# A 3 x 3 convolution on one core: a small unused load at the head is replaced by two small stores of zeros into the output

## The chip, the core and the metric

The kernel runs on one core of a Trainium2 chip. The metric is device time in microseconds (us) of that core, and less is better. Each kernel is run several times, and the median is compared. Beside the runs there is one profiled execution, whose trace is what the profile shows; its span is the stretch from its first to its last instruction, and its time also has what lies around that.

The engines are named as the profile names them: PE (matmul) and PEld (its weight loads), DVE (vector), ACT (scalar), POOL, and SP (which only issues transfers here). A transfer (DMA) is issued by SP, ACT or POOL into a queue of its own (q1, q10 and q0 in the profile), and the same 16 DMA engines carry all of them.

## The reference

```python
x_pad = np.pad(x, ((0, 0), (0, 0), (1, 1), (1, 1)))
for b, co, ci, kh, kw in all:
    output[b, co] += weight[co, ci, kh, kw] * x_pad[b, ci, kh:kh+h, kw:kw+w]
```

There are 16 images of 64 channels, 64 x 64 pixels each, and 128 output channels, all float32. The input has 16.8 MB, the output 33.6 MB, the weights 0.29 MB.

## The kernel before, in words

Images are worked on in pairs: the 64 channels of two images fill the 128 partitions, so a pair p is one input tile of 128 x 4096 elements, and there are eight pairs. Output rows are made two at a time (even row, odd row), so that they share a product: with row weights G0, G1, G2, the kernel forms G1 times the sum of two neighbouring input rows once, and adds to it (G2 - G1) and G0 products for the even row, (G0 - G1) and G2 products for the odd row. The sums of rows are tiles `ss` (L73), the 16-bit inputs are tiles `xs`.

The head, in program order: ACT's queue loads `first` (L42), 64 bytes from each of 48 rows of the input, which nothing reads. SP's queue loads the weights `w_raw` (L44), then the first pair `x0` (L46), then the second `x1` (L48). POOL makes an identity matrix, casts the weights to 16 bits (L53), and then issues the loads of pairs 2 to 7 (L59), which cast on the way. PE transposes the weights (L91); ACT and DVE make the five weight matrices `Wt` from them (L93 to L96, L100, L101). Of `x0`, DVE makes the row sums (L73) and ACT the 16-bit copy (L98); of `x1`, POOL makes the sums and ACT the copy (L174).

The main loop runs over the eight pairs and, in each, over four blocks of 16 output rows. A block has three groups of matmuls (L154) into two PSUM tiles each (one for each image): the shared product, which ACT copies to SBUF (L168), and the two others, to which DVE adds it, into the even and odd rows of an output tile `ot` (L177, L180). The output tiles share a pool of seven buffers with `x0` and `x1`. When a pair is complete, SP stores the first image (L182, in the helper at L112), and ACT, at its next turn, the second (L171). Each is 2 MB; of the last two pairs some are stored in halves.

Calls wrapped in `keep` hold their program order. The rest is placed by the tile framework, which gives each SP and ACT transfer one of eight completion semaphores in turn, and makes a transfer wait for the one eight places earlier, which used the same semaphore. It also makes a store wait for an earlier store to the same place.

Of the kernel before, what the change touches and what calls it, by code (L numbers as in the profile page):

```python
# [8 lines left out]
F32 = mybir.dt.float32  # L9
# [4 lines left out]
def kernel(  # L14
# [6 lines left out]
    nc = tc.nc  # L21
    B, CI, H, W = x.shape
# [5 lines left out]
    keep = tc.keep_in_program_order  # L28
    x_rows = x.rearrange("b c h w -> (b c) h w")
    out_rows = out.rearrange("b co h w -> b co h w")  # L30
    w_flat = weight.rearrange("co ci kh kw -> co (ci kh kw)")

    const = ctx.enter_context(tc.tile_pool(name="const", bufs=1))
# [4 lines left out]
    upool = ctx.enter_context(tc.tile_pool(name="upool", bufs=4))  # L38


    first = const.tile([48, 16], F32)
    nc.scalar.dma_start(first, x_rows[5 * 128 :: 8, 0, 0:16])  # L42
    w_raw = const.tile([CO, CI * 9], F32)
    nc.sync.dma_start(w_raw, w_flat)  # L44
    x0 = opool.tile([128, H, W], F32, tag="ot", name="x0")
    nc.sync.dma_start(x0, x_rows[0:128, :, :])  # L46
    x1 = opool.tile([128, H, W], F32, tag="ot", name="x1")
# [169 lines left out]
```

## Time and profile before

| | |
|---|---|
| median of three runs | 127.28 us (126.99 to 127.28) |
| the profiled execution, its time | 127.19 us |
| its span | 125.4 us |
| PE, DVE, ACT, POOL busy | 84%, 67%, 36%, 28% of the span |
| queues q1 (SP), q10 (ACT), q0 (POOL): packets' time, share of 16 DMA engines | 40.7%, 31.5%, 24.6% |
| HBM read and written | 17.08 MB and 33.55 MB |

The span is read together with the queues' shares, which add up to 96.8% (q8 and q14 bring 0.3% more): the 16 DMA engines are hardly ever without a packet. The chain of waits follows the end of the work back to what released it, and the windows give, for each stretch of time, what engines and DMA did there. In a window shorter than a few us the DMA share can be over 1, since a packet is counted where it starts.

### The profile page before, as it was taken

To read this page: it belongs to the slowest core of one execution; us is meant where nothing else is said; L and a number is where in the kernel's file an instruction comes from. 1 tells how busy PE (TensorE), PEld (TensorE's weight loads), DVE (VectorE), ACT (ScalarE), POOL (GpSimd) and SP (SyncE) were. 2 spreads that over 40 slices of the span, in tenths; PEclk is the share of its full clock that TensorE was granted. 3 is DMA by queue.
4 is the path that set the end of the run, shared out by engine and by line. 5 is a ranking of instruction groups with operands and counts; after the bars stand their busy time and mean duration, and the time that the engine had idled before them with its cause. 6 is when DMAs were issued, how large, how long until landed. Compare 5 with 4: busy or idle time off the path is not lost.

```text
span 125.4 us, 2409 instructions
## 1 busy us (share of the span) xinstructions
PE 105.8 (84%) x978; PEld 53.4 (43%) x978; DVE 83.5 (67%) x134; ACT 44.5 (36%) x76; POOL 34.5 (28%) x27
## 2 busy tenths in 40 slices
PE   0407999999999999999999999999999999996000
PEld 0303445554545545554554545454554555452000
DVE  0009297787778777777787778788788878868000
ACT  4108937953333333333333333333333333331000
POOL 2840008999367005700480039000000000000000
PEclk9999999999999999999999999999999999999965
DMA  5899999999999999999999999999999999999980
GB/s 160 358 355 340 324 311 212 212 209 204 366 361 374 345 350 348 355 379 350 345 361 361 418 423 423 449 423 423 434 418 418 434 426 418 431 426 426 410 371 37
DMA packets 4106, 44.48 MB, mean 355 GB/s; under 512 B 512, under 2 KB 512, under 8 KB 640
## 3 DMA queue, kind: packets, MB, share of 16 engines
q1 hardware_dynamic: 1872, 21.27, 40.7%
q10 hardware_dynamic: 1360, 16.78, 31.5%
q0 software_dynamic: 864, 6.29, 24.6%
q8 instruction: 7, 0.11, 0.3%
q14 instruction: 3, 0.02, 0.0%
HBM read 17.08 MB, written 33.55 MB: 404 GB/s over the span
## 4 chain that ended last, share of the span: by engine, by line
PE 82%; DMA 7%; DVE 2%; issue 1%; DVEq 0%; SPq 0%
PE acc L154 82%; DMA x<-in_x_dram 7%; DVE ot L177 1%; DVE ss L73 1%; DVE ot L180 0%; DVEq L212 0%; SPq L44 0%; DVEq L177 0%
## 5 line engine op out<-in xcount | busy, mean ns | idle before, releaser
L154 PE MATMUL acc<-xs,Wt 64*128 64x504 f16 (+3 forms) x768 | 88.6, 377 | 0.0
L154 PEld LDWEIGHTS <-Wt 64*128 64x128 f16 x960 | 52.3, 95 | 56.5 <-issue 6.5
L177 DVE TENSOR_TENSOR ot<-acc,ut 128x512 f32<-128x512 f32 x64 | 41.2, 686 | 23.1 <-PE acc L154 18.5
L168 ACT COPY ut<-acc 128x512 f32<-128x512 f32 x64 | 34.4, 589 | 60.6 <-issue 40.6
L180 DVE TENSOR_TENSOR ot<-acc,ut 128x512 f32<-128x512 f32 x64 | 41.1, 685 | 0.0
L73 POOL TENSOR_TENSOR ss<-xs 128x1024 f16<-128x1024 f16 x12 | 25.2, 2128 | 29.0 <-PE acc L154 25.8
L154 PE MATMUL acc<-ss,Wt 64*128 64x504 f16 (+1 forms) x192 | 27.0, 384 | 4.5 <-DVE ss L73 4.5
L73 DVE TENSOR_TENSOR ss<-x 128x512 f16<-128x512 f32 x4 | 2.6, 685 | 9.5 <-DMA x<-in_x_dram 9.5
L73 POOL TENSOR_TENSOR ss<-x 128x1024 f16<-128x1024 f32 x2 | 4.7, 2363 | 11.6 <-DMA x<-in_x_dram 11.6
L98 ACT CAST xs<-x 128x1024 f16<-128x1024 f32 (+2 forms) x4 | 4.0, 1054 | 3.9 <-DMA x<-in_x_dram 3.9
L91 PE MATMUL wp<-ident,w 128*64 128x128 f16 x18 | 1.3, 327 | 4.5 <-POOL w L53 4.5
L174 ACT CAST xs<-x 128x1024 f16<-128x1024 f32 x4 | 4.0, 1058 | 0.0
L59 POOL DMA_DIRECT2D xs<-in_x_dram x6 | 3.4, 582 | 0.0
L91 PEld LDWEIGHTS <-w 128*64 128x64 f16 x18 | 1.1, 209 | 4.5 <-POOL w L53 4.5
L93 ACT ACT_TABLE_LOAD x1 | 1.3, 1283 | 1.2 <-PEq L201 1.2
L93 ACT CAST Wt<-wp 128x384 f16<-128x384 f32 x1 | 0.5, 479 | 2.7 <-PE wp L91 2.7
L53 POOL CAST w<-w_raw 128x576 f16<-128x576 f32 x1 | 0.7, 664 | 2.4 <-DMA w_raw<-in_weight_dram 2.4
L100 ACT CAST Wt<-wp 128x384 f16<-128x384 f32 x1 | 0.5, 480 | 0.5 <-DVE Wt L96 0.5
L95 DVE TENSOR_TENSOR Wt<-wp,Wt 128x384 f16<-128x384 f32 x1 | 0.5, 549 | 0.0
L96 DVE TENSOR_TENSOR Wt<-wp,Wt 128x384 f16<-128x384 f32 x1 | 0.5, 546 | 0.0
L101 ACT CAST Wt<-wp 128x384 f16<-128x384 f32 x1 | 0.5, 484 | 0.0
masks.py:199 POOL TENSOR_SCALAR_AFFINE_SELECT ident<-ident 128x128 f16<-128x128 f16 x1 | 0.3, 295 | 0.1
(5 smaller groups left out, 0.6 us busy)
## 6 DMA issues: line engine op xcount, KB each, us to landing
out_dram<-ot ACTq DMA_DIRECT2D x7, 2048.0 KB, 20.2
out_dram<-ot SPq DMA_DIRECT2D x6, 2048.0 KB, 20.8
xs<-in_x_dram POOLq DMA_DIRECT2D x6, 1024.0 KB, 31.0
x<-in_x_dram SPq DMA_DIRECT2D x2, 2048.0 KB, 13.0
out_dram<-ot SPq DMA_DIRECT2D x4, 1024.0 KB, 10.3
out_dram<-ot ACTq DMA_DIRECT2D x2, 1024.0 KB, 9.2
w_raw<-in_weight_dram SPq DMA_DIRECT2D x1, 288.0 KB, 3.0
first<-in_x_dram ACTq DMA_DIRECT2D x1, 3.0 KB, 2.7
```

What stands on the lines that cost most here:

```text
L53: keep(nc.gpsimd.tensor_copy(w16, w_raw))
L59: keep(nc.gpsimd.dma_start(xs[p], x_rows[128 * p : 128 * p + 128, :, :]))
L73: eng.tensor_add(ss[p][:, lo : lo + n, :], v[:, lo : lo + n, 0, :], v[:, lo : lo + n, 1, :])
L91: nc.tensor.matmul(wp[q : q + 64, k * CO : k * CO + CO], w16[:, t::9], ident)
L93: keep(nc.scalar.copy(wrow(G1), wps[1]))
L95: keep(nc.vector.tensor_sub(wrow(G21), wps[2], wrow(G1)))
L98: keep(nc.scalar.copy(xs[0][:, lo:hi, :], x0[:, lo:hi, :]))
L154: nc.tensor.matmul(tiles[b2][:, lo - j0 : hi - j0, c_lo:c_hi], Wt[p0 : p0 + 64, wi, kw, :], rhs, start=i == 0, stop=i == n - 1,)
L168: keep(nc.scalar.copy(ut, U[b2]))
L174: keep(nc.scalar.copy(xs[1][:, lo : lo + 16, :], x1[:, lo : lo + 16, :]))
L177: nc.vector.tensor_add(ots[b2][:, j0 : j0 + RB, 0, :], A[b2], us[b2])
L180: nc.vector.tensor_add(ots[b2][:, j0 : j0 + RB, 1, :], Bt[b2], us[b2])
```

## The change

`first` and its load are taken out. In its place DVE writes zeros into a tile of 128 x 16 elements, and two stores take 64 bytes from each of 16 of its partitions: ACT's queue stores to every eighth channel of the last image (15), where `first` was issued; SP's queue to every eighth channel of image 14, between the weights' load and that of the first pair. Both places are written again at the end by the stores of pair 7.

```diff
-    first = const.tile([48, 16], F32)
-    nc.scalar.dma_start(first, x_rows[5 * 128 :: 8, 0, 0:16])
+    zero = const.tile([128, 16], F32)
+    keep(nc.vector.memset(zero, 0.0))
+    nc.scalar.dma_start(out_rows[B - 1, ::8, 0, 0:16], zero[0:16, :])
     w_raw = const.tile([CO, CI * 9], F32)
     nc.sync.dma_start(w_raw, w_flat)
+    nc.sync.dma_start(out_rows[B - 2, ::8, 0, 0:16], zero[16:32, :])
     x0 = opool.tile([128, H, W], F32, tag="ot", name="x0")
     nc.sync.dma_start(x0, x_rows[0:128, :, :])
```

In the order of instructions on each engine, the changed kernel has the zeros first on DVE, one store in the load's place on ACT, and one store more on SP ahead of both input loads; PE and POOL keep their rows.

## The prediction

> **What bounds the kernel now.** I read the page's slices first, then the chain of waits, then the timeline and the windows of the head. The slices:
>
> ```profile
> PE   0407999999999999999999999999999999996000
> DMA  5899999999999999999999999999999999999980
> GB/s 160 358 355 340 324 311 212 212 209 204 366 361 374 345 350 348 355 379 350 345 361 361 418 423 423 449 423 423 434 418 418 434 426 418 431 426 426 410 371 37
> ```
>
> The DMA row is to be read before PE's: the 16 DMA engines are full from the second slice to the last but two, some 6 us longer than PE at the end. (GB/s counts bytes written, so the loads of pairs 2 to 7, which shrink to 16 bits on the way, show about half of what they read.) The chain in order of time:
>
> ```profile
> 0.74 0.38 SPq L44
> ...
> 1.17 8.32 DMA x<-in_x_dram
> ...
> 9.52 0.70 DVE ss L73
> ...
> 10.26 103.36 PE acc L154 x948
> ```
>
> After `x0` has landed PE runs 103 us without a gap. So there are two long chains, PE's and that of the DMA engines, and both begin with the transfer issued at L46. Which of them ends last? The last two stores, 1 MB each, are issued at 115.59 and 116.19 and land 8.6 and 8.3 us later, while at the 430 GB/s around them 2.1 MB take 4.9 us. There are some 3 us of other stores ahead of them: the DMA engines set the end, and PE could be 2 us late without moving it. What counts is time that DMA engines lose. The head, by timeline and windows:
>
> ```profile
> 0.74 0.38 SPq L44 DMA_DIRECT2D w_raw<-in_weight_dram  x1
> ...
> 1.17 0.42 SPq L46 DMA_DIRECT2D x<-in_x_dram  x1
> ...
> 1.65 0.42 SPq L48 DMA_DIRECT2D x<-in_x_dram  x1
> ```
>
> ```profile
> 1.50:2.00 0.50, 0.00 (x0) 0.00 (x0) 0.00 (x0) 0.50 (x1) 0.00 (x0) 1.00 0.55 60
> 2.00:2.50 0.50, 0.00 (x0) 0.00 (x0) 0.00 (x0) 0.46 (x1) 0.00 (x0) 1.00 0.65 172
> 2.50:3.00 0.50, 0.00 (x0) 0.00 (x0) 0.00 (x0) 0.00 (x0) 0.00 (x0) 1.00 1.88 618
> 3.00:3.50 0.50, 0.00 (x0) 0.00 (x0) 0.00 (x0) 0.00 (x0) 0.00 (x0) 1.00 0.84 271
> 3.50:4.00 0.50, 0.00 (x0) 0.00 (x0) 0.00 (x0) 0.00 (x0) 0.25 (x1) 1.00 0.89 295
> 4.00:4.50 0.50, 0.04 (x2) 0.04 (x2) 0.00 (x0) 0.00 (x0) 0.50 (x2) 1.00 0.69 295
> ```
>
> The last two columns are DMA share and GB/s. The first bytes come about 1 us after the first issue. The weights (0.29 MB) are through near 3 us, and then `x0` moves at 271 to 295 GB/s until 4.5, while the next half us shows 492 and the stores' stretches later 430. So between 3.0 and 4.5 us the DMA engines are short of data of `x0`, and not held by the weights.
>
> **The change, part by part.**
>
> *The load at L42 goes.* 48 packets of 64 bytes, three for each DMA engine, read by nobody. Ahead of it nothing waits, and behind it on ACT stands only the table load, which ends at 2.46 while ACT's next work starts at 5.12. Worth 0; from below, the two 64-byte packets per engine that come in its place bring the balance to within 0.1 us either way (the weights' 128 packets of 2304 bytes take all engines about 1 us).
>
> *The zeros on DVE.* No DVE memset stands in the trace. The nearest rows are POOL's memsets, 0.10 us (128x1) and 0.21 us (128x128). DVE has no work before 9.52, so it costs DVE nothing; the stores wait for it. ACT, SP and POOL all start at 0.73 to 0.74, so the zeros are there by 0.83 to 0.95, and a hand-over by semaphore takes 0.05 (the cast L53 ends at 4.41, PE starts at 4.46).
>
> *ACT's store* goes out at 0.9 to 1.0 and not at 0.73. Behind it waits the table load: it ends by 2.75, still 2.4 us before 5.12. 0.
>
> *SP's store.* SP is busy with the weights until 1.12 and would issue the next at 1.17, so the wait for the zeros is over by then: 0, with 0.2 us to spare. Without that cover, each 0.1 us by which DVE starts late is 0.1 us on the next term. **The issue itself is the term**: SP issues at 0.74, 1.17 and 1.65, so one transfer takes 0.43 to 0.48 of its queue; the mean is 0.45. Both `x0` and `x1` are issued that much later. The weights are not moved, nor are POOL's loads, which hang on the weights (issued from 4.35).
>
> *Does the delay pass?* The two ends are 0 (if engines are still busy with the weights when `x0` arrives) and 0.48. The windows show `x0` short of data from 3.0 on, with no other queue that could fill in before POOL's loads arrive. I take all of it, 0.45. On PE's side `x0` may land up to 0.9 us later, as more of it runs beside POOL's loads; of the 3 us of stores queued at the end that takes a part and costs nothing more. `x1` moves with PE's chain.
>
> *The stores' waits at the end.* One transfer more turns the eight semaphores by one place; each store still waits for the transfer eight places before, the same store as now. Image 15's first half also waits for ACT's zeros, which land about 100 us earlier. 0.
>
> *The zeros in HBM.* No 64-byte store stands in the trace. From below: a gain, if something paid at the first store now is paid early (a rival, 0.70 at most). From above: SP's store stands ahead of `x0` in its queue and could hold it (a rival, 0.9). The nearest rows are the large stores: from 100 to 114 us, where one ends and the next begins again and again in both queues, the DMA share stays at 0.92 to 1.04. I take 0.
>
> Here a rule speaks against the change. The Trainium skill (DMA: Bandwidth & Descriptors, Specifications) says that a transfer below 512 bytes costs a read-modify-write, so a store of zeros would be a trip to HBM and back; no run here shows it. By that rule alone the sum would be that of the second rival. The same page (Two DMAs through the same engine are not ordered) says that descriptors of one queue start in order but are pipelined, by which the trip would not hold `x0` and the sum would stay.
>
> Sum: +0.45 us. The profiled execution has 127.19 (125.4 of span and 1.79 around it), so it would take 127.64. On the median of the runs, 0.09 higher, it is **127.7**.
>
> **The rivals.**
>
> 1. *The delay is hidden.* If the weights still occupy the engines when `x0` now arrives (issue 1.60 to 1.65, and 1.0 us to the first bytes: 2.65, where the weights end near 3), only 0 to 0.1 us is lost: 127.3. For it: the 618 GB/s at 2.5 to 3.0 show that engines pass from weights to `x0` without a hole. Against: the 1.5 us after it at under 300.
>
> 2. *The small store holds the queue.* The load `first`, with the same 64 bytes, landed 2.7 us after its issue. If `x0` has to wait for such a trip, it moves from 1.17 + 2.7 = 3.87 and not from 3.0: +0.9, or 128.2. The point from which it decides: when SP's zeros land later than about 3.4 and nothing of `x0` passes them. Against it stand the large stores above.
>
> 3. *The first store is paid early, and the kernel is not slower.* The first output stores are issued at 25.95 and 26.55, and soon after that the loads in flight slow down:
>
> ```profile
> 28.00:28.50 0.50, 0.50 (x8) 0.25 (x6) 0.50 (x2) 0.00 (x0) 0.50 (x2) 1.00 1.40 229
> 28.50:29.00 0.50, 0.50 (x8) 0.21 (x4) 0.50 (x2) 0.00 (x0) 0.50 (x1) 1.00 0.76 98
> 29.00:29.50 0.50, 0.50 (x8) 0.28 (x6) 0.50 (x2) 0.46 (x1) 0.50 (x1) 1.00 1.28 147
> 29.50:30.00 0.50, 0.50 (x8) 0.26 (x6) 0.13 (x1) 0.50 (x2) 0.50 (x1) 1.00 0.68 115
> ```
>
> From 28.5 to 30.0 they move 120 GB/s against 225 over 24 to 28: 1.5 x (1 - 120/225) = 0.70 us of DMA time. No later store shows such a dip. If that is a price of the first write into the output, the zeros pay it at the head, where the engines wait for first bytes anyway: 127.28 - 0.70 = 126.6, with the late `x0` on top 127.0. It decides if the price belongs to the engine or the whole output tensor, and not to the place that is written. Against it: it may be the mere turn from loading to storing, which zeros at the head don't take away.
>
> That the change doesn't do what it says is hardly a rival: both stores stand in the queues where the diff puts them.
>
> **How the numbers follow.** Forecast (0.2 to 0.7 us slower) 0.45; hidden 0.15; held 0.20; paid early 0.20. A measurement of this kernel can tell about 0.3%, which is 0.38 us, from no change. The forecast lies just over that, so of its 0.45 I give 0.27 to slower and 0.18 to the same; held is all slower; hidden is the same; paid early is 0.15 faster and 0.05 the same. Slower 0.47, same 0.38, faster 0.15. The range takes in the rivals' times, from 126.6 to 128.2, with 0.2 above for a hold with the late issue on top: 126.6 to 128.4. The forecast's own range is 127.5 to 128.0.
>
> **What would show it.** In the changed kernel: SP's issues near 0.74, 1.17, 1.6 and 2.1, ACT's store near 0.95; the DMA share of `x0` starting some 0.45 later; `x` landing near 9.9 to 10.4; and the dip at 28.5 still there, some 0.5 to 0.9 us later. Rival 1 would show `x0`'s bytes at the old times; rival 2 a hole of 1 us after the weights; rival 3 no dip. I would be wrong if DVE were late with the zeros, or if the order in which the queues share the engines changed and the last engine ended earlier or later by some tenths.

## The result and the profile after

The changed kernel takes 128.57 us (median of four runs, 128.33 to 129.02) against 127.17 for the kernel before: a ratio of 1.0117, 95% interval 1.0098 to 1.0137. It is 1.4 us slower, three times what was forecast and above the range. The profiled execution takes 128.33 us, its span is 126.5 us.

The slices of the kernel after, the same two rows as in the prediction:

```profile
PE   0400899999999999999999999999999999999200
DMA  4999999999999999999999999999979999999993
```

PE starts a slice later, and the DMA row, full before, has a 7 near 92 us. The chain of waits in order of time (start us, length us, what):

```profile
0.74 0.38 SPq L45
...
1.17 0.42 SPq L46
...
1.65 10.63 DMA x<-in_x_dram
...
12.30 0.70 DVE ss L75
...
13.05 103.70 PE acc L156 x948
```

SP's three issues stand where the prediction put them: weights at 0.74, zeros at 1.17, first pair at 1.65. But the first pair's transfer takes 10.63 us and not 8.32, lands at 12.28 and not at 9.49, and PE starts 2.8 us late. The head, by windows (last two columns: DMA share and GB/s):

```profile
3.00:3.50 0.50, 0.00 (x0) 0.00 (x0) 0.00 (x0) 0.00 (x0) 0.00 (x0) 1.00 1.09 315
3.50:4.00 0.50, 0.00 (x0) 0.00 (x0) 0.00 (x0) 0.00 (x0) 0.17 (x1) 1.00 0.64 197
4.00:4.50 0.50, 0.00 (x0) 0.00 (x0) 0.00 (x0) 0.00 (x0) 0.50 (x2) 1.00 0.72 295
```

At 3.5 to 4.0 this is 197 GB/s where the kernel before moved 295. But these windows count a packet where it starts, and a packet of 16 KB takes 0.6 us or more here, so that it fills one window and leaves the next one short. Counted over their whole length, the packets keep this share of the 16 DMA engines busy, by half us:

```
from us   2.0   2.5   3.0   3.5   4.0   4.5
before    0.87  0.98  1.00  1.00  1.00  1.00
after     0.95  0.91  0.70  0.81  0.88  1.00
```

So in the kernel before the engines pass from the weights to the first pair without a hole, and in the kernel after up to 30% of them stand without a packet there. The completion records of the first pair show what became of it. Each of the 16 DMA engines reports its own share; in us from the span's start, sorted:

```
before  8.29 8.47 8.54 8.56 8.59 8.63 9.16 9.20 9.21 9.26 9.26 9.29 9.29 9.30  9.36  9.49
after   8.40 8.66 8.85 9.26 9.32 9.41 9.43 9.44 9.48 9.50 9.53 9.63 9.69 10.07 12.22 12.28
```

Place by place in this order, fourteen are 0.1 to 0.8 us later than before; the last two are almost 3 us later, and PE waits for the last. Engines that land far behind the others I call **stragglers**. Late in the kernel, windows of before and then of after:

```profile
92.00:93.00 1.00, 1.00 (x12) 0.50 (x10) 1.00 (x3) 0.00 (x0) 0.00 (x0) 1.00 0.97 410
93.00:94.00 1.00, 1.00 (x12) 0.53 (x10) 0.66 (x2) 0.93 (x2) 0.00 (x0) 1.00 1.04 442
...
104.00:108.00 4.00, 4.00 (x40) 1.95 (x37) 3.27 (x6) 1.07 (x2) 0.00 (x0) 1.00 1.04 436
```

```profile
92.00:93.00 1.00, 1.00 (x12) 0.49 (x10) 1.00 (x3) 0.00 (x0) 0.00 (x0) 1.00 0.80 328
93.00:94.00 1.00, 1.00 (x12) 0.53 (x10) 0.67 (x2) 0.97 (x2) 0.00 (x0) 1.00 0.47 197
...
104.00:108.00 4.00, 4.00 (x42) 2.08 (x40) 3.42 (x6) 1.07 (x2) 0.00 (x0) 1.00 0.89 363
```

With PE 3 us late, the stores come 3 us late (SP's at 93.11, before at 89.98), the queued stores are used up, and the DMA engines stand partly idle at 92 to 94 and again before 108: the holes are 0.2 + 0.5 us and 0.4 us. Counted as above, in the mean of the 16 engines, the idle time is 0.3 us more than before in the first 8 us and 1.1 us more from 88 to 118, and the last transfer ends 1.3 us later. (Two further differences nearly cancel: the packets take 0.6 us more in all, and after 118 us the engines idle 0.8 us less.) So the smaller part of the price is paid at the head, and the larger part when the stores run out, because PE started late.

### The profile page after: what moved, and what is told of

Read it like the earlier page. It is cut to its first block, busy times and chain, and to the rows that moved or that the text cites. A ratio compares the mean times of both kernels' runs of the same rounds, so it can differ in the third digit from the quotient of the medians.

```text
span 126.5 us, 2412 instructions
## 1 busy us (share of the span) xinstructions
PE 106.2 (84%) x978; PEld 53.1 (42%) x978; DVE 83.7 (66%) x135; ACT 44.5 (35%) x76; POOL 34.5 (27%) x27
## 4 chain that ended last, share of the span: by engine, by line
PE 82%; DMA 8%; DVE 2%; issue 1%; SPq 1%; DVEq 0%
PE acc L156 82%; DMA x<-in_x_dram 8%; DVE ot L179 1%; DVE ss L75 1%; DVEq L214 0%; DVE ot L182 0%; SPq L46 0%; SPq L45 0%; DVEq L179 0%
```

## The experiments

The kernel before was run beside each group; its median was 127.11 to 127.19 there. The ratio and its 95% interval are taken from the single runs and need not be the quotient of the two medians. "Spread" is the time from the first to the last of the 16 engines' completions of the first pair, in the run's profiled execution.

**Which part costs?** First the parts of the change one by one. Neither load nor stores:

```diff
-    first = const.tile([48, 16], F32)
-    nc.scalar.dma_start(first, x_rows[5 * 128 :: 8, 0, 0:16])
```

> Neither the unused load nor any store of zeros. Theory 'held' (SP's store of zeros holds the first pair's queue on some DMA engines, the first pair lands 2.8 us late, and PE's chain with it): the time of before, 127.1 to 127.4, first pair landing near 9.5. Theory 'load' (the unused load made something at the head or later faster, and its loss is the cost): 128.2 to 128.8, with no store at all. Theory 'issue' (only the later issue by SP costs): 127.1 to 127.4.

127.21 us, ratio 1.0010 (0.9988 to 1.0032), first pair at 9.62. The unused load is worth nothing. ACT's store alone in its place:

```diff
+    zero = const.tile([128, 16], F32)
+    keep(nc.vector.memset(zero, 0.0))
+    nc.scalar.dma_start(out_rows[B - 1, ::8, 0, 0:16], zero[0:16, :])
```

> The unused load is replaced by ACT's store of zeros alone; SP's queue is as before. Theory 'held': 127.1 to 127.6, since nothing stands ahead of the first pair in SP's queue; first pair landing 9.4 to 9.8. Rival 'any store' (a small write into HBM at the head holds the DMA engines whichever queue it is in): 128.0 to 128.8, the first pair landing after 11. Theory 'issue': 127.2.

127.25 us, ratio 1.0006 (0.9980 to 1.0031). So a write into HBM at the head costs nothing by itself. Its profiled execution, at 128.25 the slowest of ten, happened to have one straggler, which landed at 12.51 with the other fifteen by 9.64: stragglers also occur now and then with an early issue. SP's store alone, the unused load kept:

```diff
     nc.sync.dma_start(w_raw, w_flat)
+    nc.sync.dma_start(out_rows[B - 2, ::8, 0, 0:16], zero[16:32, :])
```

> The unused load stays; SP's store of zeros stands between weights and first pair. Theory 'held': the time of the changed kernel, 128.2 to 128.9, with the first pair landing near 12 and a few DMA engines 2 us behind the rest. Theory 'load': 127.2. Theory 'issue': 127.6 to 128.0 at first pair landing near 10 to 10.4.

129.19 us (two of the ten runs at 127.6 and 127.7, the others from 128.8 to 129.7), ratio 1.0125 (1.0084 to 1.0166), first pair at 12.83: the whole price, and a little more than I had expected. So far this is what "held" expects. But a load in the same place:

```diff
     nc.sync.dma_start(w_raw, w_flat)
+    small = const.tile([16, 16], F32)
+    nc.sync.dma_start(small, x_rows[5 * 128 :: 24, 0, 0:16])
```

> As the run before, with a load of 64 bytes from each of 16 rows in the place of SP's store (nothing reads it): the same issue on SP, the same packets, no write into HBM. Theory 'held': only the issue is paid, 127.2 to 127.7, the first pair landing 9.8 to 10.4. Theory 'issue' (any instruction there costs it all, because the first pair meets more of POOL's loads): 128.2 to 128.8 and a landing near 12.

129.46 us (four runs: 127.70, 129.53, 129.39, 129.70), ratio 1.0134 (1.0047 to 1.0222). The same price with no write into HBM, so "held" by a store fell. The profiled execution is the mild one of the four, 127.70, with the first pair at 10.77 and a spread of 1.3.

**Is it the transfer or the time of issue?** The store behind the two input loads:

```diff
     nc.sync.dma_start(x1, x_rows[128:256, :, :])
+    nc.sync.dma_start(out_rows[B - 2, ::8, 0, 0:16], zero[16:32, :])
```

> The unused load stays, and SP's store of zeros is issued behind the two input loads. Theory 'late issue' (what costs is that the first pair is issued 0.45 us later and then meets POOL's loads; what the extra transfer is does not matter): the time of before, 127.0 to 127.4, the first pair landing near 9.5. Rival 'extra transfer' (one more transfer in SP's queue at the head costs wherever it stands): 128 or more.

127.01 us, ratio 0.9980 (0.9962 to 0.9998): free, and 0.2% below the kernel before at the edge of its interval. Then no added transfer at all, only a later issue (the three loads are kept in program order):

```diff
+    keep(nc.vector.memset(x0[:, 0:12, :], 0.0))
-    nc.sync.dma_start(x0, x_rows[0:128, :, :])
+    keep(nc.sync.dma_start(x0, x_rows[0:128, :, :]))
```

> No transfer is added; SP issues the first pair about 0.5 us later, because DVE first writes zeros into a part of its buffer (the load then overwrites them). Theory 'late issue': the time of the run with a small load on SP, 128.5 to 129.5 in most executions, the first pair landing at 10.5 to 13. Rival 'extra transfer' (the packets or the completion of the small transfer hold the queue): 127.5 to 127.7, the first pair landing near 10.

129.13 us, ratio 1.0144 (1.0107 to 1.0181). Timeline and chain of this kernel:

```profile
0.74 0.38 SPq L44 DMA_DIRECT2D w_raw<-in_weight_dram  x1
0.97 0.70 DVE L46 MEMSET x<- 128x768 f32 x1 [0.97 <-PEq L202]
1.69 0.33 SPq L47 DMA_DIRECT2D x<-in_x_dram  x1
```

```profile
1.69 11.10 DMA x<-in_x_dram
...
12.90 0.70 DVE ss L74
13.64 103.81 PE acc L155 x948
```

Half a us of delay, with not one packet more, gives 2 us and a spread of 3.6. **A later issue is enough**, and the store only brings it about.

**Do POOL's loads make it so dear?** They arrive from 8 us on and share the engines with what is left of the first pair. Changed kernel and kernel before, with these loads behind the first pair's landing:

```diff
+    seen = const.tile([128, 16], F32)
+    keep(nc.gpsimd.tensor_copy(seen, x0[:, 0, 0:16]))
     for p in range(2, NP):
         load(p)
```

> The changed kernel, with POOL's loads of pairs 2 to 7 issued only when the first pair has landed (a small POOL copy reads it first). Theory 'met by POOL's loads' (a DMA engine that starts the first pair late must share with these loads, and each late packet counts double): the first pair lands at 8.6 to 9.6, and the time comes back to 127.0 to 127.7. Rival 'held' (the engines themselves stand still at the head): landing after 10.5 even so, and 128.2 or more.

> The kernel before with the same wait of POOL's loads. Theory 'met by POOL's loads': the first pair lands near 8.3 and not 9.5; PE starts 1.2 us earlier; the DMA engines stay full with the second pair until the loads come, so the time is the same or up to 0.5 us less, 126.6 to 127.3. Rival: the loads come too late and the engines stand still, 127.5 or more.

The changed kernel stays at 128.98 us (127.80 to 129.53), ratio 1.0116 (1.0071 to 1.0162); the kernel before is unmoved, 127.14, ratio 1.0005 (0.9984 to 1.0026), its first pair at 8.82 with a spread of 0.5 (I had expected 8.3), and PE 0.7 us earlier. In the changed kernel's profiled execution (128.23) the first pair lands at 10.29 and PE starts at 11.06, 2 us earlier than without the wait; the spread is 1.7. So the late issue spreads the landings even without these loads (1.7 against 0.5), and sharing with them makes it more (3.9 against 1.2). Sharing does lengthen the last landing, but taking it away doesn't bring the time back. That theory fell too.

**How does the price grow with the delay?** Less delay, by a shorter write of zeros (7 rows in the place of 12):

> As the run with the late issue, with a shorter write of zeros: the first pair is issued near 1.4 and not 1.69 (before: 1.17). Theory 'ran empty' (the price comes when DMA engines have finished the weights, near 3.0, before the first pair has reached them; an engine that has run empty starts late by 1 us or more, and PE starts with the last of them): the price is no straight line in the delay, 127.2 to 128.0 here against 129.1 for twice the delay, since most engines are still at the weights. Rival 'each tenth costs' (any delay is multiplied by four on its way to the end): 128.0 to 128.4.

Issue at 1.36: 127.18 us, ratio 1.0006 (0.9983 to 1.0030). The engines stay as full as before (0.98 or more from 2.5 on). The first 0.2 us are free, and the next 0.3 cost 2 us. More delay (22 rows):

> The first pair is issued near 2.3 us, the weights at 0.74 as before. Theory 'issued under traffic': the cost does not grow in line with the delay; the first pair's way is as slow as at 1.69 or, when the weights are already through, faster again: last landing 11 to 13.5, 129 to 130. Rival 'each tenth costs' (four times the delay): 131 or more.

Issue at 2.36: 128.36 us, ratio 1.0094 (1.0081 to 1.0107), spread 0.7. Later is cheaper than at 1.69. I had expected 129 to 130 and a landing after 11: the landing came at 11.20, the time below my interval. Its cost, 1.17 us, is the 1.19 us of delay and no more.

**Have the engines run empty?** The late issue, and a second load of the weights on ACT's queue to keep them busy; then that load alone:

```diff
-    first = const.tile([48, 16], F32)
-    nc.scalar.dma_start(first, x_rows[5 * 128 :: 8, 0, 0:16])
+    first = const.tile([CO, CI * 9], F32)
+    nc.scalar.dma_start(first, w_flat)
```

> The late issue (1.69), and in the place of the unused load a second, unused load of all the weights by ACT's queue, so that the DMA engines have work until about 3.7. Theory 'ran empty': the engines pass from weights to first pair without a hole, all land close together (within 1.2 us), at 9.3 to 10.2; 127.5 to 128.2, of which 0.7 is the second load's own time. Rival 'late is late' (the engines are not the point, the first pair's own way to them is slow when it is issued late): 129.2 to 130, landing spread over 3 us.

> The control for the run above: the second load of the weights by ACT, the first pair issued at 1.17 as in the kernel before. Both theories: 0.3 MB more at 430 GB/s is 0.7 us of the DMA engines, 127.4 to 128.0, the first pair landing at 9.6 to 10.4.

The control is as expected: 127.85 us, ratio 1.0046 (1.0026 to 1.0066), spread 1.2. With the late issue it is the worst of all, 129.79, ratio 1.0211 (1.0167 to 1.0255):

```profile
1.69 12.54 DMA x<-in_x_dram
...
14.33 0.70 DVE ss L74
```

Its 16 engines land from 10.45 to 14.23, as the rival 'late is late' had it. The second load did not keep the engines busy: from 3.75 to 4.75 us they are 46% busy, and 100% in the control. With more traffic ahead, the first pair came to them later still. That an engine starts late because it has run empty, as the theory said, doesn't hold either: with the issue at 2.36 the engines are only 12% busy from 3.0 to 3.5, and all land within 0.7. Idle engines are what a late arrival leaves behind, and not why it is late. What the kernels with stragglers had in common was that the weights were about to move when the first pair was issued: it was issued at 1.64 to 1.69, and the weights' first bytes come at 1.75.

**Is it the traffic, or a fixed time in the head?** Everything later by 0.75 us, the order and the distances kept, the unused load left out:

```diff
+    keep(nc.vector.memset(w_raw[:, 0:576], 0.0))
-    nc.sync.dma_start(w_raw, w_flat)
+    keep(nc.sync.dma_start(w_raw, w_flat))
```

> Weights, first and second pair are all issued about 0.75 us later (weights near 1.5, first pair near 1.95), since DVE first writes zeros into the weights' buffer; the unused load is left out. Between weights and first pair stand the usual 0.45 us. Theory 'issued under traffic' (a transfer issued when no data moves yet is at the engines in 1.0 to 1.6 us, one issued once the weights are moving needs 2 to 4 us on some engines): no stragglers, landings within 1.3 us of each other, the last near 10.2, and 127.7 to 128.2, the plain delay. Rival 'a fixed event after 1.4 us' (the table load of ACT, 1.2 to 2.5, or something else that stands at a fixed time in the head): stragglers as with the late issue, 129.3 or more.

127.82 us, ratio 1.0062 (1.0043 to 1.0082):

```profile
1.49 0.38 SPq L43
...
1.92 8.23 DMA x<-in_x_dram
...
10.18 0.70 DVE ss L72
...
10.92 103.17 PE acc L153 x948
```

The first pair is issued at 1.92, later than in the late-issue run, and lands at 10.15 with a spread of 1.2; the weights' first bytes come only at 2.51 here. Against the late-issue run, this is 1.3 us less for 0.23 us more of delay. And the first pair late at 1.69, with the weights behind it:

> The first pair is issued at 1.69 as in the run with the late issue, but nothing moves then: the unused load is left out and the weights are issued behind it (near 2.1). The time says little, since the weights land behind the first pair and PE waits for them. Theory 'issued under traffic': the first pair's 16 engines land within 1.3 us of each other, the last at 8.3 to 9.2, earlier than in the kernel before though issued 0.5 us later. Rival 'a fixed event after 1.4 us': landings spread over 2 us or more.

Landings from 8.88 to 9.45, a spread of 0.6 (the last a little later than I had said); 128.16 us, ratio 1.0082 (1.0066 to 1.0097), since here PE waits for the weights. A fixed event in the head is excluded; ACT's table load, the one candidate, still runs at the issue in both (0.73 to 2.02).

**Does it hold for the change itself?** Both stores of zeros in place, SP's now ahead of the weights:

```diff
-    nc.sync.dma_start(w_raw, w_flat)
     nc.sync.dma_start(out_rows[B - 2, ::8, 0, 0:16], zero[16:32, :])
+    nc.sync.dma_start(w_raw, w_flat)
```

> The changed kernel with one swap: SP's store of zeros is issued ahead of the weights and not behind them. The first pair is then issued later than in the changed kernel (near 1.85 and not 1.65), but 0.45 us behind the weights, so before these move. Theory 'issued under traffic': no stragglers, the first pair lands at 9.6 to 10.4, 127.4 to 127.9: of the change's 1.4 us only the plain delay is left. Rival 'late by the clock' (what counts is how late the first pair is issued): 128.6 or more.

127.59 us (127.40 to 127.74), ratio 1.0044 (1.0029 to 1.0059):

```profile
0.91 0.38 SPq L45
1.34 0.41 SPq L46
...
1.81 8.41 DMA x<-in_x_dram
...
10.24 0.70 DVE ss L75
```

The first pair is issued 0.16 us later than in the changed kernel and lands 2.1 us earlier. Of the change's 1.4 us the plain delay is left, 0.48. The zeros' own bytes move at 1.79 to 1.98 here, just as the first pair is issued, and do no harm. SP's zeros land 1.4 us after their issue, where behind the weights they took 2.9.

**A better version?** The first pair on ACT's queue at once, the unused load left out:

```diff
-    first = const.tile([48, 16], F32)
-    nc.scalar.dma_start(first, x_rows[5 * 128 :: 8, 0, 0:16])
+    nc.scalar.dma_start(x0, x_rows[0:128, :, :])
```

> A version that may beat both: the unused load goes, and ACT's queue issues the first pair at once, at 0.73, beside the weights on SP. Theory 'ran empty': the engines never run empty at the head, and PE may start up to 0.3 us earlier, but the DMA engines set the end: 126.8 to 127.2. Rival: the weights, now sharing with the first pair, land late (after 4.5) and POOL's loads with them: 127.2 to 127.6.

127.24 us, ratio 0.9988 (0.9965 to 1.0011), the same; the weights land after 8 us and PE starts later, at 11.51, at no cost. Of all these kernels only the one with the store behind the input loads has an interval that lies below 1, by 0.0002; none is clearly better than the kernel before.

The first pair in the kernels that bear on this, by the profiled execution, beside the median of the runs. The two idle columns are the mean idle time of the 16 engines, in us, in two stretches of the span:

```
kernel                  first bytes   issue of     last      spread  idle   idle      median
                        of weights    first pair   landing           3:5    88:118    us
before                  1.75          1.17          9.49     1.2     0.0    0.0       127.2
issue 0.2 later         1.76          1.36          9.44     1.2     0.0    0.0       127.2
small load              1.75          1.64         10.77     1.3     0.1    0.6       129.5
the change              1.75          1.65         12.28     3.9     0.3    1.1       128.6
SP's store alone        1.75          1.65         12.83     4.2     0.3    1.6       129.2
late issue              1.76          1.69         12.80     3.6     0.5    1.5       129.1
late, more traffic      1.75          1.69         14.23     3.8     0.7    1.7       129.8
still later             1.75          2.36         11.20     0.7     0.8    0.4       128.4
all late                2.51          1.92         10.15     1.2     0.0    0.0       127.8
store ahead of weights  2.39          1.81         10.21     1.2     0.0    0.1       127.6
```

The row of the small load is its mild execution, of 127.70 us. In the five kernels with an issue at 1.64 to 1.69, 27 of 30 runs take 128.3 us or more and three take 127.55 to 127.70; the kernel before takes at most 128.13 in the 97 runs beside the experiments. So the time of issue makes stragglers very likely, and not certain.

## Why the prediction was wrong

**What bounds the kernel**: that the DMA engines set the end was right in the main, and both chains do start with the first pair. But "PE could be 2 us late without moving it" was read off the last two stores alone. With PE 2.8 us late, the windows at 92 to 94 us show the stock of waiting stores used up long before the end; and with PE 1.8 us late (issue at 2.36) the engines already idle for 0.4 us from 88 to 118.

**The parts priced at nothing** were right: the lost load (1.0010), the memset (0.07 us, done at 0.88), ACT's store (1.0006). Nothing of the stores' waits shows at the end of the chain.

**The issue of SP's store**: its own length was right (0.48 between the issues). Where no engine straggles, a delay passes for the most part, as the sum had it: 0.48 us for 0.6 with the store ahead of the weights, 0.63 for 0.75 with everything late, 1.17 for 1.19 with the first pair issued at 2.36.

**"Does the delay pass? The two ends are 0 and 0.48"** is the step that failed, in three places. First, its reading was wrong: "`x0` short of data from 3.0 on" came from windows that count a packet where it starts. Counted over their length, the packets keep the engines full from 2.5 on, so there was room for a small delay, and the first 0.2 us of it are free.

Second, it took a transfer's way to the engines as fixed, so that a later issue could cost at most its lateness. The runs show that this way depends on when the transfer is issued, measured from the weights' first bytes at 1.75. Issued at 1.36 or before, the first pair costs nothing more; at 1.64 to 1.69 it comes late to a few engines, which land up to 3 us behind. The term of 0.45 measures 1.4 in the change and 2 us where nothing but the issue is later (129.13).

Third, it let `x0` land "up to 0.9 us later" at no cost on PE's side. That the loads of pairs 2 to 7 meet the late engines was in that figure and is true, but it was priced by the mean of the engines, while PE waits for the last. The landing is 2.8 us later, the stores run out, and that is the larger part of the price: 1.1 us of idle engines from 88 to 118, against 0.3 at the head.

**The rivals**: "the delay is hidden" had the right ground, engines that pass from the weights to `x0` without a hole, and holds for the issue at 1.36; at 1.65 it fails, because the 1.0 us to the first bytes isn't that of every engine. "The small store holds the queue" came nearest in time (128.2) and by its sign, a hole after the weights; its mechanism is wrong, since a small load and even no transfer do the same. By the Trainium skill (DMA: Bandwidth & Descriptors, Specifications) a transfer below 512 bytes does a read-modify-write; such stores on ACT's queue alone leave the time unmoved (ratio 1.0006), and in SP's queue store and load of the same size measure 129.19 and 129.46, so nothing of it is seen in the time. "Paid early" is wrong: the dip at the first output stores is still there, 3 us later, in windows of the kernel after:

```profile
30.00:31.00 1.00, 1.00 (x12) 0.51 (x10) 0.76 (x2) 0.07 (x1) 1.00 (x2) 1.00 0.98 197
31.00:32.00 1.00, 1.00 (x13) 0.51 (x10) 1.00 (x2) 0.00 (x0) 1.00 (x2) 1.00 1.33 188
32.00:33.00 1.00, 1.00 (x13) 0.45 (x11) 0.75 (x2) 0.83 (x2) 1.00 (x1) 1.00 0.85 115
```

Zeros at the head take nothing from it.

**What stays open**: by what way a transfer issued just before another starts to move comes late to some engines. The runs show when it happens, not how. They can't tell the weights' first bytes from the weights' issue, which is 1.0 us earlier in all of them, and no run issues the first pair late on another queue than the weights'. A straggler can also come with an early issue, as with ACT's store alone. With POOL's loads held back PE starts 2 us earlier and the engines no longer run dry from 88 to 118, yet the time hardly changes; the engines still idle 0.5 us more at the head than in the kernel before and their packets take 0.65 us more in all, and why they do is not settled. That an engine which starts late stays late, since each carries its own share of every transfer, fits this (the second pair's last two completions, at 21.98 and 22.11, are as far behind the other fourteen as the first pair's), but no run tests it.

## What to carry to other kernels

At the head of a kernel, issue the transfer that the first work waits for well before the bytes of a large transfer ahead of it begin to move, even if something small has to go behind it or ahead of both: here an issue 0.4 us before them was free, and one 0.1 us before them cost 1.4 to 2 us. Read the completion of each DMA engine, not only the landing of the transfer: PE waits for the slowest of 16. Don't read a shortage out of windows that are shorter than a packet. A small transfer costs by the place it takes in the issue order of its queue, and not by its bytes: 2 us between the weights and the first pair, 0.5 us ahead of both, nothing behind the input loads.

## What the runs showed of the hardware

- The first bytes come 0.9 to 1.0 us after the issue of the first transfer (0.74 to 1.75; 1.49 to 2.51 when all is late; 0.91 to 1.79 for the zeros ahead of the weights).
- A first pair issued just before the weights' first bytes (1.64 to 1.69 against 1.75) lands on the 16 engines over 3.6 to 4.2 us in four of six profiled executions; the other two are the small load's mild one (1.3) and the change with POOL's loads held back (1.7). Issued 0.4 us or more before these bytes it lands over 0.5 to 1.5 (ACT's store alone had one straggler, and 4.2); with nothing moving over 0.6; 0.6 us after they started over 0.7.
- A store of 16 x 64 bytes into HBM lands 2.8 to 3.0 us after its issue when it goes next after the weights, on either queue, and 1.4 to 1.5 us after it when it goes first. A load of 48 x 64 bytes beside the weights lands after 2.7 us in the kernel before.
- DVE's memset of 128x16 takes 0.07 us, of 128x768 0.70 us.
